# An encoder layer on one core: where w_out's operands, the second norm's vectors and the second gate's row are formed, and two operands kept as halves

## The chip, the cores and the metric

The kernel runs on one core of one Trainium2 chip. The metric is the device time of one execution in microseconds, median of several runs.

## The reference

One layer of a bidirectional encoder, in float32, over 2048 tokens of width 1024, and a final norm. Cut to what matters here:

```python
mod = silu(c) @ w_mod + b_mod                      # c: (1, 1024); w_mod: 1024 x 6144
shift1, scale1, gate1, shift2, scale2, gate2 = split(mod, 6)

h = rms_norm(x, g_norm1) * (1 + scale1) + shift1
q_a, k_a, v_a, q_m, k_m, v_m, o_m, gates = split(h @ w_in, ...)
att = rms_norm(banded_attention(q_a, k_a, v_a, sink), g_attn_out)      # 8 heads, window 128
q_m, k_m = split(silu(conv3(concat([q_m, k_m]))))
h_m = mlstm forward + mlstm backward               # 4 heads of 128, chunks of 128
h_m = sigmoid(o_m) * rms_norm(h_m, g_mlstm_out)
x = x + gate1 * (concat([att, h_m]) @ w_out)       # w_out: 1024 x 1024

hff = rms_norm(x, g_norm2) * (1 + scale2) + shift2
a, b = split(hff @ w_ffn_in, 2)                    # 1024 x 5632
x = x + gate2 * ((silu(a) * b) @ w_ffn_out)        # 2816 x 1024
return rms_norm(x, g_final)
```

## The kernel before

**Numbers as halves.** Every large product is made of three matmuls: each operand is split into a high half (rounded by ACT) and a low half (the difference, by DVE), and hi x hi, hi x lo and lo x hi are summed (`mm3`, L54 to L58). Splitting an operand of 128x1024 is one ACT and one DVE instruction. The projections through w_out and the two products of the feed-forward are written as 2 x 2 blocks with seven products instead of eight, so their operands are sums and differences of blocks, numbered 0 to 6.

**The stages, in order of time** (us of the profiled execution):
- 0 to 182, first stage: the first norm of x, 128 tokens at a time (`tt` 0 to 15), turned into `hT`; `nat_mm` computes the values and gate columns (`pa`, `pv`) of one tile in 48 matmuls. Beside this the modulation vectors are made. `mod_row(m)` sums the 1024 rows of a block of w_mod on DVE (`macc`, L373 and L375, from `wmod` tiles), splits the sum (L141, L142), adds over the partitions with two matmuls by ones (`modrow`, L381, L382), and either writes a row to memory (m = 2 and 5, the gates, into `gate_d`) or picks the columns out with DVE (m = 3 and 4, for the second norm). Row 2 is made beside tiles 4 to 7, rows 3 to 5 beside tiles 8 to 15 and behind them.
- 182 to 245, conv stage: columns of w_in (`w_first`, `w_second`, then `next_cols`) are loaded to `wraw`, split into `w0h`/`w0l` or `w1h`/`w1l` (ACT L251, POOL L254) and multiplied with hT (`gps`, L498). Two generators run beside it: `gates` (the mLSTM's gates, whose small matmuls are put at the 36th, 66th and 90th `gps` matmul by its `yield`s) and `w_out_ops`: for 8 pieces of w_out it loads two tiles, multiplies them with gate1 (POOL L944, L946), forms four differences (POOL L957) and stores the seven operands to `wo_d`.
- 245 to 570, mLSTM: for each of 4 heads a backward pass over 15 chunks and a forward pass over 16. Each chunk calls `tick()`, which runs what was put into `later` when its count is down. `prep(cc)` adds a mask on POOL (L629), `decays` takes exponentials on ACT, `k_chunk` makes `kn` and `vw`, and `kv_mm` is the product `kvp` (L622). The rest of PE's time goes to projection matmuls from the queue `fill` (`pull`).
- 570 to 815, attention, with the last projections between.
- 815 to 1004, output projection: 8 pairs of 128 tokens, each seven products of 4 steps of three matmuls (`out_proj`, `ops`). For the pair two ahead, `square` forms sums of squares (ACT L1075, POOL L1076, L1077), `columns` sums them over the partitions on PE (`aps`, L1125), `diagonal` and `scale` (PE L1088, DVE L1092) normalise the attention half, `gate` and `sums` form the operands, and `hi` and `lo` split them (L1114, L1118). w_out's operands are fetched with `start_wo(u)` (L1042) and split with `finish_wo(u)` (L1046, L1047), those of products 5 and 6 during the first pair (L1516, L1519). Behind a product DVE adds its bank to the residual (L1224).
- 1004 to 2267, feed-forward and final norm: 44 units of 84 matmuls, then the product with w_ffn_out.

**What sets the order.** PE's order is the program's from the start. In the first stage the other engines' order is made by the framework's planner from its own costs; from the conv stage to the end of the first phase of w_ffn_out it is the program's on all of them (`manual_schedule`), except in the attention. All large transfers go through SP's queue, in order, and an issue that must wait holds those behind it. A tile with one buffer under a tag is reused when its readers and its stores are done.

Of the kernel before, what the change touches and what calls it, by code (L numbers as in the profile page):

```python
# [11 lines left out]
F32 = mybir.dt.float32  # L12
# [24 lines left out]
def hybrid_layer_kernel(  # L37
# [35 lines left out]
    wo_d = dp.tile([7, 4, P, 512], F32, name="wo_d")  # L73
    a_d = dp.tile([7, DFF // P // 2, P, 2, 512], F32, name="a_d")
# [70 lines left out]
    xs, s2s = ExitStack(), ExitStack()  # L145
# [132 lines left out]
    with tc.tile_pool(name="sw", bufs=2, side="right", reuse_waits="tile") as sw:  # L278
# [80 lines left out]
        def mod_row(m):  # L359

            for z in range(2):
                acc = sw.tile([P, 512], F32, tag="macc", name="macc", bufs=1)
                if m in (2, 5):
                    br = (s1 if m == 2 else wp).tile([1, 512], F32, tag="mrow" if m == 2 else "oth", name="brow", bufs=1)
                    sp.dma_start(br, b_mod[:, m * D + z * 512:m * D + (z + 1) * 512])
                for k in range(0, KT, 2):
                    w = (hp if "b" in wrow[0] else sw if "m" in wrow[0] else wp).tile([P, 2, 512], F32, tag=wrow[0], name="wmod", bufs=1)
# [15 lines left out]
                if m in (2, 5):  # L383
                    dve.tensor_tensor(br, ps[:1, :], br, ADD)
                    sp.dma_start(gate_d[m // 5:m // 5 + 1, z * 512:(z + 1) * 512], br)
                    continue
                row = sw.tile([P, 512], F32, tag="macch", name="mrow", bufs=1)
                act.activation(row, ps, AF.Copy)
                for k in range(4):
                    rk = row[:, k * P:(k + 1) * P]  # L390
                    dve.tensor_tensor_reduce(out=rk, in0=rk, in1=ident, op0=MUL, op1=ADD, scale=1.0, scalar=0.0,
                                             accum_out=mod[:, m, 4 * z + k:4 * z + k + 1])
            if m not in (2, 5):
                o = O_BM + m * KT
                dve.tensor_tensor(mod[:, m, :], mod[:, m, :], cols[:, o:o + KT], ADD)
# [48 lines left out]
        for n in range(NB):  # L444
# [11 lines left out]
            if n + 1 == NB:  # L456
                w_first = proj_cols(C_KM)
            for i in range(4):
                tt = 4 * n + i
                if tt < 3:  # L460
# [7 lines left out]
                if tt == 8:  # L468
                    deque(nrm, 0)
                    wrow = deque(["w1h", "w1l", "wm0", "wm1"])  # L470
# [3 lines left out]
                    vecs = chain.from_iterable(mod_row(m) for m in range(3, 6))  # L474
# [9 lines left out]
                if tt != 9:  # L484
                    next(vecs, None)
# [1478 lines left out]
```

## Time and profile before

| | |
|---|---|
| median of 3 runs | 2265.35 us (2265.24 to 2266.26) |
| profiled execution | 2268.64 us |
| its span | 2266.8 us |
| PE busy | 2223.8 us, 98% |
| DVE, ACT, POOL busy | 71%, 47%, 46% |
| moved by DMA | 391 MB, 173 GB/s |

One execution is profiled; times count from the start of its span. A line of the list of waits reads: engine, tile and line that waited, `<-` what ended the wait, then the total in us, how often, and the longest. A line of the timeline reads: start, length, engine, line, operation, output `<-` inputs, shape, and in brackets how long the engine had been idle and what released it. A released-by is inferred from the latest of the events that an instruction waited for.

### The profile page before, as it was taken

What the parts mean: (1) busy time and instruction counts of PE and PEld (TensorE: products, weight loads), DVE (VectorE), ACT (ScalarE), POOL (GpSimd) and SP (SyncE); (2) the same over time, 40 slices, a digit from 0 to 9 for tenths busy, and PEclk for the clock granted to TensorE, in tenths of its full rate; (3) what the DMA queues carried; (4) which work ended last, traced back from release to release, by engine and by line L of the source; (5) the groups of instructions that cost most, each with busy time, mean ns of one, the idle gap of its engine ahead of it and who ended that gap; (6) DMA issues with size and microseconds to landing.
All of it is one profiled execution on the core that took longest, in us unless ns stands there. A gap on an engine that the chain in (4) does not pass through costs nothing.

```text
span 2266.8 us, 32424 instructions
## 1 busy us (share of the span) xinstructions
PE 2223.8 (98%) x10822; PEld 1858.7 (82%) x10822; DVE 1611.1 (71%) x2944; ACT 1060.3 (47%) x2206; POOL 1040.6 (46%) x914
## 2 busy tenths in 40 slices
PE   6999999999999999999999999999999999999998
PEld 4997888888888878888888888888888888878887
DVE  6787577656688877886767786766666665785694
ACT  5433565654677746354444444433333333233452
POOL 1006635334344333436666674457566654692020
PEclk9999999999999999999999999999999999999999
DMA  8476755586666576764343454433333374542462
GB/s 329 161 244 209 246 166 168 182 240 180 205 186 183 174 243 207 268 235 150 108 149 112 158 181 164 157 98 111 98 112 98 112 260 142 176 142 94 144 217 93
DMA packets 352811, 391.28 MB, mean 173 GB/s; under 512 B 21260, under 2 KB 251004, under 8 KB 352644
## 3 DMA queue, kind: packets, MB, share of 16 engines
q1 hardware_dynamic: 352420, 389.18, 52.6%
q8 instruction: 85, 1.39, 0.2%
q14 instruction: 82, 0.67, 0.1%
q10 hardware_dynamic: 224, 0.04, 0.0%
HBM read 269.95 MB, written 119.19 MB: 172 GB/s over the span
## 4 chain that ended last, share of the span: by engine, by line
PE 88%; DVE 4%; ACT 3%; DMA 2%; issue 1%; POOL 1%; SPq 0%; ACTq 0%; POOLq 0%; DVEq 0%
PE gps L498 14%; PE fp L56 12%; PE fp L57 12%; PE fp L58 12%; PE fo L56 6%; PE fo L58 6%; PE fo L57 6%; PE ops L56 2%; PE ops L58 2%; PE ops L57 2%; PE kvp L622 1%; PE num L709 1%; PE num L711 1%; PE atp L805 1%; ACT ap L788 1%
## 5 line engine op out<-in xcount | busy, mean ns | idle before, releaser
L498 PE MATMUL gps<-hT,whi 128*128 128x512 f32 x1088 | 396.5, 419 | 0.3 <-DVE cacc L513 0.3
L56 PE MATMUL fo<-w,ah 128*128 128x512 f32 x616 | 239.9, 389 | 1.0 <-DVE rb L1876 1.0
L58 PE MATMUL fo<-w,al 128*128 128x512 f32 x616 | 239.9, 389 | 0.1
L57 PE MATMUL fo<-w,ah 128*128 128x512 f32 x616 | 239.7, 389 | 0.0
L498 PE MATMUL gps<-hT,wlo 128*128 128x512 f32 x544 | 226.7, 417 | 0.0
L498 PEld LDWEIGHTS gps<-hT,whi 128*128 128x128 f32 x1088 | 200.2, 190 | 24.7 <-DVE cacc L513 0.7
L56 PE MATMUL fp<-T,S 128*128 128x512 f32 x528 | 206.7, 391 | 0.3 <-ACT s L1610 0.3
L57 PE MATMUL fp<-T,S 128*128 128x512 f32 x528 | 205.6, 389 | 0.0
L58 PE MATMUL fp<-T,S 128*128 128x512 f32 x528 | 205.4, 389 | 0.0
L1718 DVE TENSOR_TENSOR al<-al,ah 128x1024 fp32r<-128x1024 f32 x77 | 117.4, 1530 | 108.0 <-ACT ah L1717 108.0
L1717 ACT ACTIVATE ah<-al 128x1024 fp32r<-128x1024 f32 x77 | 81.6, 1060 | 182.8 <-DMA al<-a_d 180.3
L1453 DVE TENSOR_TENSOR S<-sf,S 128x512 fp32r<-128x512 f32 x86 | 129.8, 1547 | 34.4 <-ACT S L1452 34.2
L1453 DVE TENSOR_TENSOR A<-graw,A 128x512 fp32r<-128x512 f32 x86 | 130.8, 1541 | 13.2 <-ACT A L1452 12.8
L58 PE MATMUL fp<-B,A 128*128 128x512 f32 x352 | 136.9, 389 | 0.0
L56 PE MATMUL fp<-B,A 128*128 128x512 f32 x352 | 136.9, 389 | 0.0
L57 PE MATMUL fp<-B,A 128*128 128x512 f32 x352 | 136.9, 389 | 0.0
L56 PEld LDWEIGHTS fo<-w,ah 128*128 128x128 f32 x616 | 115.6, 188 | 25.4 <-DVE rb L1876 1.8
L58 PEld LDWEIGHTS fo<-w,al 128*128 128x128 f32 x616 | 115.6, 188 | 24.7 <-DVE al L1718 0.5
L57 PEld LDWEIGHTS fo<-w,ah 128*128 128x128 f32 x616 | 115.6, 188 | 24.2
L1620 DVE SCALAR_TENSOR_TENSOR g<-t,g 128x512 f32<-128x512 f32 x44 | 41.8, 950 | 131.3 <-ACT t L1619 131.3
L798 POOL TENSOR_SCALAR ap<-ap,adn 128x384 f32<-128x384 f32 (+1 forms) x128 | 73.5, 594 | 125.7 <-PE atp L805 58.6
L1457 POOL TENSOR_TENSOR sf<-A,A22r 128x512 f32<-128x512 f32 x42 | 58.1, 1383 | 145.5 <-DMA A22r<-in_w_ffn_in_dram 118.5
(427 smaller groups left out, 6142.2 us busy)
## 6 DMA issues: line engine op xcount, KB each, us to landing
al<-a_d SPq DMA_DIRECT2D x77, 512.0 KB, 3.8
wmod<-in_w_mod_dram SPq DMA_DIRECT2D x48, 512.0 KB, 7.6
graw<-in_w_ffn_in_dram SPq DMA_DIRECT2D x43, 512.0 KB, 3.9
a_d<-ka SPq DMA_DIRECT2D x66, 256.0 KB, 4.7
bc<-bc_d SPq DMA_DIRECT2D x64, 256.0 KB, 3.7
hop_d<-n SPq DMA_DIRECT2D x56, 256.0 KB, 4.0
a_d<-u SPq DMA_DIRECT2D x55, 256.0 KB, 4.6
mqk<-qk_d SPq DMA_DIRECT2D x44, 256.0 KB, 3.8
```

The costliest lines, as they stand in the source:

```text
L56: pe.matmul(o, lh, rh, start=first, stop=False, skip_group_check=skip)
L57: pe.matmul(o, lh, rl, start=False, stop=False, skip_group_check=skip)
L58: pe.matmul(o, ll, rh, start=False, stop=last, skip_group_check=skip)
L498: pe.matmul(ps, w[i == 2][:, k, :], hT[n](i == 1, k), start=(k == 0 and i == 0), stop=(k == KT - 1 and i == 2))
L622: pe.matmul(kvp[:, :129], kn, vw, start=True, stop=True)
L709: pe.matmul(num[:, d, :129], sc[:, d, :], va_c, start=True, stop=st is None)
L798: pool.tensor_scalar(self.p[g][:, :self.NK], self.p[g][:, :self.NK], dn[:, g:g + 1], 0.0, MUL, ADD)
L1453: dve.tensor_tensor(t[:, 1, :], f, t[:, 0, :].bitcast(F32), SUB)
L1457: add.tensor_tensor(f1, a21, a22, ADD)
L1620: dve.scalar_tensor_tensor(g0, t0, 1.0, g0, ADD, MUL)
L1717: act.activation(ah, al.bitcast(F32), AF.Copy)
L1718: dve.tensor_tensor(al, al.bitcast(F32), ah.bitcast(F32), SUB)
```

## The change

It moves three pieces of work and rearranges what they touch.

- **w_out.** `w_out_ops` moves from the conv stage into the first stage, beside tiles 9 to 12, in four rounds over full rows instead of eight over half rows. It uses the tags of the projection weights: w_out rows in `wm0`/`wm1` (even rounds) and `w0h`/`w0l` (odd rounds), the differences in `w1h` (`ta`) and `w1l` (`tb`). The gain `g_attn_out` is multiplied into w_out's rows here (ACT), so `scale` in the output projection no longer has it. `w_first` is emitted at tile 14 instead of 12.
- **Halves.** The operands of products 4 and 6 are split before they are stored (a high half in `wo_d`, a low half in the new `wol_d`), and are loaded as two halves. The order of loads and splits before and in the first pair of the output projection changes with it, the squares are taken at step 9 instead of 15, and the pool `xd` opens at step 22 instead of 14.
- **The second norm's vectors** (rows 3 and 4) are formed in the mLSTM, a quarter row at a time: `late_vecs` loads 128x2x256 pieces into the tag `oth`, sums on DVE four ticks later, and `vec_columns` does the two matmuls, of 256 columns. `prep(0)` and `prep(1)` move from the end of the backward pass into its chunks 3 and 1.
- **The second gate's row** (row 5) is formed by `gate2` in the feed-forward's second half, one step in each unit.
- The steps of `gates` are put at matmul 46, 80 and 104 instead of 36, 66 and 90.

```diff
-            vecs = chain.from_iterable(mod_row(m) for m in range(3, 6))
+            wx = wxs.enter_context(tc.tile_pool(name="wx", bufs=1, side="left", reuse_waits="tile"))
+            gb = wx.tile([P, 2, 512], F32, name="gb")
+            sp.dma_start(gb.rearrange("p m c -> p (m c)"), gate_d[0, :].partition_broadcast(P))
+            vecs = w_out_all()
...
+        def w_out_ops(k, b):
+            bx, by = b
+            act.activation(bx, bx, AF.Copy, scale=cols[:, O_GA + k:O_GA + k + 1])
+            for t in (bx, by):
+                pool.tensor_tensor(t, t, gb, MUL)
+            ta = wp.tile([P, 2, 512], F32, tag="w1h", name="ta", bufs=1)
+            tb = wp.tile([P, 2, 512], F32R, tag="w1l", name="tb", bufs=1)
+            hi = wx.tile([P, 2, 512], F32R, name="tbh")
+            tf = tb.bitcast(F32)
+            sp.dma_start(wo_d[0, k], bx[:, 0])
+            sp.dma_start(wo_d[1:6:4, k].rearrange("u p c -> p u c"), by)
+            for t, f, g in ((ta[:, 1], bx[:, 1], bx[:, 0]), (tf[:, 0], by[:, 1], bx[:, 1]),
+                            (ta[:, 0], by[:, 1], ta[:, 1]), (tf[:, 1], by[:, 0], ta[:, 0])):
+                pool.tensor_tensor(t, f, g, SUB)
+            sp.dma_start(wo_d[2:4, k].rearrange("u p c -> p u c"), ta)
+            act.activation(hi, tf, AF.Copy)
+            dve.tensor_tensor(tb, tf, hi.bitcast(F32), SUB)
+            sp.dma_start(wo_d[4:7:2, k].rearrange("u p c -> p u c"), hi.bitcast(F32))
+            sp.dma_start(wol_d[:, k].rearrange("u p c -> p u c"), tf)
+
+        def w_out_load(k):
+            r = [pl.tile([P, 2, 512], F32, tag=tag, name="wox", bufs=1)
+                 for pl, tag in (((sw, "wm0"), (sw, "wm1")), ((wp, "w0h"), (wp, "w0l")))[k % 2]]
+            for t, k_ in zip(r, (k, k + 4)):
+                sp.dma_start(t, w_out[k_ * P:(k_ + 1) * P].rearrange("p (m c) -> p m c", m=2))
+            return r
+
+        def w_out_all():
+            b = [w_out_load(0), w_out_load(1)]
+            for k in range(4):
+                yield True
+                w_out_ops(k, b[k])
+                if k < 2:
+                    b.append(w_out_load(k + 2))
...
+    def late_vecs():
+        for m in (3, 4):
+            for q in range(4):
+                acc = s2.tile([P, 256], F32, tag="lacc", name="lacc", bufs=1)
...
+                for k in range(0, KT, 2):
+                    w = wp.tile([P, 2, 256], F32, tag="oth", name="wmod", bufs=1)
+                    sp.dma_start(w, w_mod[k * P:(k + 2) * P, m * D + q * 256:m * D + (q + 1) * 256]
+                                 .rearrange("(k p) c -> p k c", p=P))
+                    yield 3
+                    for i in range(2):
+                        if k + i == 0:
+                            dve.tensor_scalar(acc, w[:, 0, :], sc_col[:, 0:1], None, MUL)
+                        else:
+                            dve.scalar_tensor_tensor(acc, w[:, i, :], sc_col[:, k + i:k + i + 1], acc, MUL, ADD)
+                split(acc, hi, lo)
+                later.append([1, lambda m=m, q=q, hi=hi, lo=lo: vec_columns(m, q, hi, lo)])
...
+            if cc in (3, 1):
+                prep(1 - cc // 2)
...
-        prep(0)
-        prep(1)
         decays(0)
...
-            for k in range(4):
-                dve.scalar_tensor_tensor(self.a[:, :, k], self.a[:, :, k], cols[:, O_GA + k:O_GA + k + 1], rb, MUL, MUL)
+            dve.tensor_tensor(self.a, self.a, rb.unsqueeze(2).to_broadcast([P, 2, 4, P]), MUL)
...
-    finish_wo(2)
     finish_fill(lasts[2])
-    for u in (4, 5):
-        start_wo(u)
-    xr.append(load_xr(nxt.tt + 1))
+    start_wo(5)
+    nx2.load_gate()
     nx3.load_a()
-    finish_wo(3)
+    xr.append(load_xr(nxt.tt + 1))
+    start_wo(4)
+    finish_wo(2)
     pull(26)
     for _ in range(2):
         nxt.both()
-    finish_wo(4)
+    finish_wo(3)
...
+    HI0, LO0 = (5, 13, 18, 20, 22, 24, 26), (5, 15, 18, 20, 22, 24, 26)
...
-                if i in (6, 14):
-                    for hi, lo in zip(*wo[5 + i // 14]):
+                if i == 6:
+                    for hi, lo in zip(*wo[5]):
                         act.activation(hi, lo.bitcast(F32), AF.Copy)
-                if i in (8, 16):
-                    for hi, lo in zip(*wo[4 + i // 8]):
-                        dve.tensor_tensor(lo, lo.bitcast(F32), hi.bitcast(F32), SUB)
-                if i in (3, 12, 13):
+                if i in (8, 11):
+                    hi, lo = (t[i // 11] for t in wo[5])
+                    dve.tensor_tensor(lo, lo.bitcast(F32), hi.bitcast(F32), SUB)
+                if i in (0, 2, 13):
                     cur.both()
-                if i == 14:
+                if i == 22:
...
-                if i == (1 if p else 15):
+                if i == (1 if p else 9):
...
+        def gate2():
+            row = lambda n, dt=F32: ff.tile([P, D], dt, tag="xt", name=n, bufs=4)
...
+            for k in range(KT):
+                if k + 1 < KT:
+                    fetch(k + 1)
+                if k == 0:
+                    dve.tensor_scalar(acc, wr[0], sc_col[:, 0:1], None, MUL)
+                else:
+                    dve.scalar_tensor_tensor(acc, wr[k % 2], sc_col[:, k:k + 1], acc, MUL, ADD)
+                yield True
```

More of the change, by code (lines that the diff above doesn't have):

```diff
@@ L967, in hybrid_layer_kernel @@
     w_second = proj_cols(C_QM)
     win = ExitStack()
-    steps = [gates(), w_out_ops()]
-    due = [0, next(steps[1])]
+    steps = [gates()]
+    due = [0]
     win.enter_context(tc.manual_schedule(engines={getattr(mybir.EngineType, e) for e in ("DVE", "Activation", "Pool", "SP")}))
@@ L1248, in hybrid_layer_kernel @@
         start_wo(u)
+    xr = [load_xr(nxt.tt)]
+    nx2.load_m()
     pull(10)
@@ L1525, in hybrid_layer_kernel @@
             if nx2:
-                if i == (1 if p else 15):
-                    sq = [xd.tile([P, 512], F32, tag="n2", name="msq", bufs=9).rearrange("p (k t) -> p k t", k=4) for _ in range(2)]
+                if i == (1 if p else 9):
+                    sq = [(xd.tile([P, 512], F32, tag="n2", name="msq", bufs=9) if p else
+                           w1.tile([P, 512], F32, tag="sq", name="msq")).rearrange("p (k t) -> p k t", k=4) for _ in range(2)]
                     for j in range(2):
@@ L1696, in beside @@
                     norms.popleft()
+                if n > NJ and u == 1:
+                    next(gate, None)
             pair(hh, j, ws_, hop, start, beside, turn)
```

165 lines of the change are left out of this document (73 added, 92 removed).

## The prediction

> **What bounds the kernel now.** I read the page first, then PE's busy time and granted clock by stretch, then the list of waits of PE, then the instructions around each place where PE stands.
>
> ```profile
> span 2266.8 us, 32424 instructions
> PE 2223.8 (98%) x10822; PEld 1858.7 (82%) x10822; DVE 1611.1 (71%) x2944; ACT 1060.3 (47%) x2206; POOL 1040.6 (46%) x914
> ```
>
> PE is busy for 2223.8 of 2266.8 us, so 43 us are all that can be won without taking matmuls away, and the change takes few away. The profiled execution took 2268.64 us, of which 2266.8 are span; the median of the runs shown is 2265.35, 3.3 us less. I make the sum as a difference and put it on the median.
>
> ```profile
> 123.00:175.00 52.00, 50.63 (x328) 48.60 (x327) 43.44 (x102) 13.54 (x30) 4.34 (x10) 1.00 0.89 284
> 175.00:182.00 7.00, 5.02 (x27) 4.32 (x26) 3.81 (x8) 2.51 (x5) 2.08 (x3) 1.00 0.39 113
> 182.00:186.00 4.00, 4.00 (x12) 3.11 (x11) 2.56 (x7) 2.35 (x5) 1.26 (x2) 0.57 0.46 148
> 245.00:570.00 325.00, 322.88 (x1892) 276.79 (x1891) 219.26 (x769) 182.45 (x580) 139.12 (x186) 1.00 0.63 189
> 815.00:828.00 13.00, 13.00 (x60) 10.61 (x59) 11.71 (x16) 5.00 (x8) 1.60 (x2) 1.00 0.92 311
> 828.00:841.00 13.00, 8.22 (x26) 6.08 (x25) 9.59 (x22) 6.44 (x11) 8.16 (x7) 0.74 0.17 50
> 1000.00:2000.00 1000.00, 999.61 (x4437) 826.47 (x4436) 695.35 (x667) 402.63 (x675) 611.96 (x385) 1.00 0.42 140
> ```
>
> The columns after the length are busy time and count of PE, PEld, DVE, ACT and POOL, then the granted clock, the DMA share and GB/s. Two places that the change touches are poor: the end of the first stage (175 to 186, with a clock of 0.57 behind the stand) and the first pair of the output projection (828 to 841: 26 matmuls in 13 us at 0.74, where 815 to 828 has 60). The feed-forward, 1000 to 2000, has PE idle for 0.4 us in 1000.
>
> ```profile
> PE aps L1125 <- POOL msq L1077: 3.2, 2, 2.1
> PE modrow L381 <- ACT macch L141: 2.2, 2, 1.6
> PE ops L56 <- ACT msq L1075: 1.6, 1, 1.6
> PE kvp L622 <- ACT vw L617: 1.2, 1, 1.2
> ```
>
> The largest of these waits behind the start-up are those of `modrow` in the first stage, one of `kvp` in the mLSTM, and `aps` and `ops` in the projection. The change edits the cause of each.
>
> **A: the first stage.** The sums for modulation rows 3 to 5 leave tiles 9 to 15, six pairs of `modrow` matmuls and their waits with them.
>
> ```profile
> 137.45 0.40 PE L381 MATMUL modrow<-macch,ones_r 128*128 128x512 f32 x1
> 137.91 0.29 PE L56 MATMUL pa<-wnh,hT 128*128 128x272 f32 x1
> 138.04 0.28 PE L57 MATMUL pa<-wnl,hT 128*128 128x272 f32 x1
> 145.12 0.39 PE L381 MATMUL modrow<-macch,ones_r 128*128 128x512 f32 x1
> 181.72 0.93 PE L498 MATMUL gps<-hT,whi 128*128 128x512 f32 x2
> ```
>
> A pair in a full stream costs 137.91 - 137.45 = 0.46 us. A tile without one takes 145.12 - 137.91 = 7.21 us, and five tiles follow 137.45, so PE could be done with the stage at 137.45 + 5 x 7.21 = 173.5, and begin `gps` there: 8.1 us before 181.6 (181.72 less the two gate transposes). Without a stand the clock would be kept too: the 12 matmuls of 182 to 186 took 4.0 us at 0.57 and take 12 x 0.225 = 2.7 at the spacing of 1000 to 2000 (4437 in 1000 us), 1.3 less.
>
> What decides is when `gps` gets its first weights. They use the tags `w0h` and `w0l`, in which the change now holds the w_out rows of k = 3, so w_first waits for the last round of `w_out_ops`. It was free of that before.
>
> ```profile
> L944 POOL TENSOR_TENSOR bx<-bx,gb 128x512 f32<-128x512 f32 x8 | 11.3, 1407 | 12.2 <-DMA bx<-in_w_out_dram 6.4 <-PE gps L498 5.8
> 189.07 1.30 POOL L944 TENSOR_TENSOR bx<-bx,gb 128x512 f32<-128x512 f32 x1 [5.80 <-PE gps L498]
> L254 POOL TENSOR_TENSOR wlo<-wraw,whi 128x256 fp32r<-128x256 f32 x68 | 51.0, 772 | 45.9 <-ACT whi L251 35.6 <-PE kvp L622 9.7 <-DMA qst_d<-qhi 0.3
> 178.79 1.06 ACT L251 ACTIVATE whi<-wraw 128x1024 fp32r<-128x1024 f32 x1 [0.32 <-DMA wraw<-in_w_in_dram]
> 830.92 1.21 DVE L1519 TENSOR_TENSOR wo<-wo 128x1024 fp32r<-128x1024 f32 x1
> wmod<-in_w_mod_dram SPq DMA_DIRECT2D x48, 512.0 KB, 7.6
> wo_d<-ts SPq DMA_DIRECT2D x8, 256.0 KB, 4.4
> 123.75 0.94 SPq L369 DMA_DIRECT2D wmod<-in_w_mod_dram  x2
> ```
>
> A round on POOL is two products of 128x1024 (2 x 1.30 less a little, 2.55 each) and four differences of 128x512 (1.30 each): 10.3 us. Single buffers link the rounds: the second difference writes `tb`, which is free when the round before has split it (ACT 1.06, DVE 1.21) and its store has landed (L). So a round takes the larger of 10.3 and 3 x 1.30 + 1.06 + 1.21 + L = 6.2 + L. With L = 4.4 that is 10.6, with 7.6 it is 13.8. I take L = 6.0, between, because the stage now moves some 17 MB (4.2 of w_out, 0.5 of the gate, 9.4 of stores, about 3 of the rest) where 123 to 175 moved 14.8 at a share of 0.89. Rounds are 12.2 us.
>
> The rows and the gate (1.57 MB, 5.5 us at 284 GB/s) are issued where the first `wmod` of this part was, at 123.75, and are there at 129.3; with ACT's scaling (1.06) POOL begins at 130.4 and ends round 0 at 140.7, round 3 at 140.7 + 3 x 12.2 = 177.3. `whi` can be made a little before that, the first quarter of `wlo` takes 0.77 more: `gps` at 178.1, 4.6 us behind PE's end of the stage. So **A = 178.1 - 181.6 = -3.5 us**, with the lower clock behind the stand as before. Its ends: -9.4 (no stand, clock kept) and, for rounds bound by slow stores, the rival below. Behind w_first stands w_second, whose slots `w1h` and `w1l` are the last round's `ta` and `tb`; it has 96 matmuls, 22 us, of cover. The gate chain's steps are put 10 to 14 matmuls later, 3 us, and the mLSTM, which reads its result, begins at about 245; that costs nothing.
>
> The row for 182 to 186 shows the clock low behind a stand in which the longest listed wait is 1.6 us. The Trainium skill (TensorE: Matmul & The Clock Gate, Part 1) has the clock halved after an idle window of about 3.4 us; by it a stand short of that would keep the clock, and A would gain up to 1.3 us more, an estimate. The trace has it halved behind less, so the sum does not use it.
>
> What leaves the conv stage with `w_out_ops` (POOL, SP) was beside PE; no gain is booked.
>
> **B: the first pair of the projection.**
>
> ```profile
> 815.16 2.35 DVE L1047 TENSOR_TENSOR wo<-wo 128x1024 fp32r<-128x1024 f32 x2
> 819.31 1.65 DVE L1092 SCALAR_TENSOR_TENSOR ma<-ma,cols,arb 128x256 f32<-128x256 f32 x4
> 829.14 0.39 PE L58 MATMUL ops<-wo,mS 128*128 128x512 f32 x1
> 828.71 1.69 DVE L1118 TENSOR_TENSOR mA<-mm,mA 128x512 fp32r<-128x512 f32 x2 [0.62 <-ACT mA L1114]
> 830.32 0.67 DVE L1224 TENSOR_TENSOR xr<-xr,ops 128x512 f32<-128x512 f32 x1
> 831.14 0.47 PE L56 MATMUL ops<-wo,mS 128*128 128x512 f32 x1 [1.61 <-ACT msq L1075]
> 832.79 1.32 POOL L1077 TENSOR_TENSOR msq<-msq 128x128 f32<-128x128 f32 x1
> 834.16 0.58 PE L1125 MATMUL aps<-ones_r,msq 128*128 128x1 f32 x2 [2.09 <-POOL msq L1077]
> 816.42 2.58 SPq L1042 DMA_DIRECT2D wo<-wo_d  x2
> ```
>
> PE stops at step 20 (product 5 into the bank of product 3). The wait is put down to ACT's `msq`, but what it needs is DVE's addition of product 3, which reads that bank: it begins at 830.32, ends at 830.99, and PE goes on at 831.14. DVE was late because it splits wo[4] (2.35 us, from 815.16) in the same queue. Then PE stops twice for POOL's `msq`, made from squares put at step 15. After the change wo[4] and wo[6] come from memory as halves, so 2.35 us go from ahead of that addition and another pair of splits from behind it; `scale` is one instruction of 1024 columns (about 1.21 for 1.65); the second operand's low half (about 0.85 of 1.69) stands behind the addition. 2.35 + 0.4 + 0.85 = 3.6 us earlier: it ends near 827.4, before PE is ready for it (829.14 + 0.23). The squares are at step 9 and out of `xd`'s way, six steps of 0.69, 4 us, earlier, and POOL has little else there (1.60 us busy in 815 to 828). So both waits go, and the lower clock with them. 828 to 841 holds 22 matmuls of 0.23 and 4 short ones of 0.15, 5.7 us of work in 13: **B = -7.3 us**.
>
> What could be late next is data: two operands' loads are doubled, 2.1 MB more, 6.7 us at the 311 GB/s of 815 to 828. wo[6] is issued at 816.4; with a landing of 7.6 and those 6.7 it is there by 830.7; PE, on time, needs it at step 24, 829.37 + 4 x 0.69 + 0.6 = 832.7. Two us are left.
>
> **C and D: the mLSTM and the feed-forward.**
>
> ```profile
> 340.47 0.73 POOL L254 TENSOR_TENSOR wlo<-wraw,whi 128x256 fp32r<-128x256 f32 x1 [9.71 <-PE kvp L622]
> 341.16 1.42 POOL L629 TENSOR_TENSOR ng<-bc,maskb 128x256 f32<-128x256 f32 x2
> 343.14 0.49 PE L622 MATMUL kvp<-vw,kn 128*128 128x129 f32 x2 [1.22 <-ACT vw L617]
> 342.73 0.42 DVE L681 SCALAR_TENSOR_TENSOR sc<-sps,ng 128x256 f32<-128x256 f32 x1 [1.91 <-ACT ng L635]
> ```
>
> The wait of 1.22 us at a head's turn is a chain: `ng` on POOL stands behind a `wlo`, ACT's exponentials behind `ng`, `vw` behind those, PE behind `vw`. `prep` is now made several chunks earlier: **C = -1.2 us**.
>
> Rows 3 and 4 now run in quarters: 8 pairs of matmuls over 256 columns in a stage where PE is 99% busy. A pair costs between 0.26 (two matmuls of 272 columns, 138.04 - 137.91 = 0.13 apart) and the 0.46 of a 512-column pair; nearest is between, 0.33: +2.6. Row 5 is two pairs of 512 columns in the feed-forward, +0.9. **D = +3.5 us** (2.9 to 4.6).
>
> DVE gets 64 products of 128x256 (0.42 each, 27 us) and some 10 us of splits and reductions in 325 us: from 219 to 256 us busy, 79%. Each product waits for a transfer of 256 KB issued four ticks earlier, and behind it on DVE stand the state updates on which PE waits two chunks later; SP has 32 more issues among the mLSTM's own. I book **+0.5 us**, ends 0 and 8. The eight products of 128x1024 in the feed-forward, 1.21 each, one in each block of 84 matmuls (19.4 us), fall where DVE has 30% free and PE waits for nothing: 0.
>
> **The sum.** -3.5 - 7.3 - 1.2 + 3.5 + 0.5 = -8.0 us: 2260.6 for the profiled execution, 2257.4 on the median.
>
> **The rivals.** No stand in the first stage: rounds at 10.6 us, as with L = 4.4, end at 172.5, the weights are there at 173.3, A is -9.4 and the time 2251.5. For it: the 4.4 row. Against: the stage's DMA share of 0.89.
>
> Slower: the rounds are bound by their stores. The sum is zero where `gps` starts 4.5 us later than before, at 186.1, which is rounds of 14.9 us, L = 8.7. At L = 11 rounds are 17.2, round 3 ends at 192.3 and `gps` starts at 193.1, 11.5 late: -7.3 - 1.2 + 4.0 + 11.5 = +7.0, 2272.4. For it: 7.6 us of landing for `wmod`, and more bytes now. Against: the bytes needed by then, 15.5 MB without the last round's stores, at the 319 GB/s that a full share makes of 284, have gone by 172. Two engines also get in each other's way: L944 has a mean of 1.41 us where one undisturbed takes 1.30. The Trainium skill (SBUF — State Buffer, Who interferes with whom) says that a VectorE instruction with two SBUF inputs and a GpSimd one that reads SBUF exclude each other for a whole instruction; were each of a round's six operations held up by one of 0.67 us, rounds would be 14.3, `gps` would start at 188.4, and the sum would be +2.3, an estimate. The trace bears out a tenth of that, and VectorE's sums leave the stage.
>
> The wait in the projection only moves: wo[6] lands 3 to 4 us late or DVE's queue is still behind at step 20, so that B is -3.5 and the time 2261.2. For it: DVE is busy for 11.71 of 13 us there.
>
> That the mLSTM's late products hold DVE for their transfers: 32 waits, half of them with 0.5 us on PE, +8, time 2264.9.
>
> **How the numbers follow.** Forecast 0.50; no stand 0.16; slow stores 0.15; moved wait 0.12; mLSTM waits 0.07. A difference of 0.2% is 4.5 us, so faster means below 2260.8 and slower above 2269.9; that is about what a measurement here can tell. Faster: 0.46 of the forecast's 0.50 (the rest has larger rounds), 0.16, and 0.05 of the moved wait: 0.67. Slower: 0.13 of the slow stores and 0.03 of combinations: 0.16. Same: 0.17. The range is from the first rival's time, less 1, to 2267, which leaves out the slow stores beyond L = 9.
>
> **What would show it.** Right: `gps` L498 starts between 173.5 and 180; no PE wait for `ops` or `aps` in the first pair and a clock of 1.00 there; no 1.2 us wait of `kvp`; the busy time of PE in the mLSTM up by some 3 us. Wrong: `gps` standing behind `whi` or `wlo` beyond 186, DVE's addition of product 3 still ending after PE's step 19, or DVE waiting for `wmod` in the mLSTM with PE behind it.

## The result and the profile after

The changed kernel takes 2306.39 us (median of 5 runs, 2301.69 to 2308.62), the kernel before, beside it, 2266.26 us: a ratio of 1.0174, 95% interval 1.0163 to 1.0186. It is 40 us slower where 8 us faster was forecast. The profiled execution took 2303.5 us.

The first two lines of its page, then busy time and granted clock by stretch, with the columns of the prediction's table:

```profile
span 2301.7 us, 32337 instructions
PE 2230.5 (97%) x10830; PEld 1864.5 (81%) x10830; DVE 1612.6 (70%) x2953; ACT 1062.3 (46%) x2217; POOL 1042.0 (45%) x890
```
```profile
123.00:175.00 52.00, 39.70 (x247) 39.07 (x246) 9.92 (x15) 12.37 (x22) 40.97 (x28) 0.87 0.74 262
190.00:245.00 55.00, 55.00 (x247) 44.80 (x246) 27.96 (x64) 24.08 (x53) 8.55 (x12) 1.00 0.28 89
250.00:610.00 360.00, 334.70 (x1896) 282.79 (x1895) 261.52 (x874) 184.32 (x589) 137.87 (x179) 0.98 0.62 190
856.00:869.00 13.00, 13.00 (x60) 10.69 (x59) 9.46 (x11) 5.73 (x9) 3.70 (x4) 1.00 1.02 356
869.00:882.00 13.00, 12.59 (x59) 9.89 (x59) 10.05 (x25) 4.80 (x9) 6.70 (x5) 1.00 0.73 242
1040.00:2040.00 1000.00, 999.52 (x4437) 826.68 (x4436) 701.60 (x676) 401.68 (x674) 618.81 (x388) 1.00 0.43 144
```

PE's busy time is 6.7 us more and the span 34.9. The first pair of the output projection, 13 us with 26 matmuls before, now has 59. The mLSTM, which had PE idle for 2.1 of 325 us, has it idle for 25.3 of 360, with a clock of 0.98, which is some 7 more, an estimate (2% of 360). In the first stage PE stands for 12.3 us.

Three rows of PE by tile mark the stages: the first `gps`, the first `kvp` and the last `num` (behind the counts: least, median and greatest duration in ns, first and last start).

```profile
L525 PE MATMUL gps<-hT,whi x1088: 387/395/778, 188.8 to 856.2; 128*128 128x512 f32 x182
L691 PE MATMUL kvp<-vw,kn x240: 271/274/581, 250.0 to 601.6; 128*128 128x129 f32 x120
L778 PE MATMUL num<-mv,sc x256: 271/273/422, 274.1 to 609.8; 128*128 128x129 f32 x128
```

Cut at these marks, and at the first `fp` of the feed-forward, every kernel of this study splits into five stretches (us, from the profiled execution of each):

| kernel | first gps | conv | mLSTM | num to fp | from fp | span |
|---|---|---|---|---|---|---|
| before | 181.7 | 63.6 | 322.4 | 422.9 | 1276.2 | 2266.8 |
| changed | 188.8 | 61.2 | **359.8** | 416.6 | 1275.3 | 2301.7 |
| difference | +7.1 | -2.4 | **+37.4** | -6.3 | -0.9 | +34.9 |

Each figure is of one execution. Ten kernels of this study share the changed kernel's first stage: nine have `gps` at 188.7 to 189.7 and one at 192.3. The stretch from `fp`, the same in all the changed kernels, varies by 3.5 us. So a few us in one stretch can be chance; the conv stage, 61.2 us in all nine kernels that have it as changed, is steadier.

Who waits for whom in the changed kernel: PE's own waits, and between 250 and 610 us those of ACT, DVE and SP's queue behind them (in total, times, longest).

```profile
PE kvp L691 <- ACT vw L686: 14.4, 8, 4.8
PE pa L56 <- ACT va L509: 12.3, 2, 10.9
PE ktp L681 <- DMA mqk<-qk_d: 5.0, 3, 2.4
PE ops L56 <- ACT mA L1137: 1.4, 1, 1.4
```
```profile
ACT lhi L142 <- DVE lacc L638: 22.8, 8, 4.5
DVE lacc L638 <- DMA wmod<-in_w_mod_dram: 6.8, 5, 2.9
```
```profile
SPq L631 <- DVE sc L750: 42.2, 11, 7.1
SPq L631 <- DVE lacc L638: 28.4, 11, 7.0
SPq L631 <- DVE cb L731: 20.6, 8, 4.1
SPq L631 <- DMA wmod<-in_w_mod_dram: 15.8, 10, 2.9
```

`aps` is gone from PE's list and `ops` has 1.4 us left, in another pair. Two new things stand out in the mLSTM. ACT waits 8 times, once for each quarter row, to split a sum that DVE has not finished. PE stands right behind every one of these: four times at `kvp` (11.6 of the 14.4 us), once for 1.9 us at `ktp` and three times for under 1 us. The other four waits of `kvp`, 2.8 us, are not behind a split. And SP's queue stands 107 us at the load of `wmod` (L631). Such a sum is no price: in the kernel before, SP stands 100.6 us at the loads of `bc` (L603), and PE is idle for 2.1 us in that whole stage. This is the largest of ACT's eight stands, engine by engine:

```profile
398.04 0.69 ACT L806 ACTIVATE og<-htp,gml 128x512 f32<-128x512 f32 x1 [1.24 <-PE htp L804]
401.23 0.35 DVE L789 TENSOR_SCALAR hst<-num,rd 128x128 f32<-128x128 f32 x1
401.88 1.28 DVE L638 SCALAR_TENSOR_TENSOR lacc<-wmod,sc_col,lacc 128x256 f32<-128x256 f32 x2
403.20 0.42 ACT L142 ACTIVATE lhi<-lacc 128x256 fp32r<-128x256 f32 x1 [4.48 <-DVE lacc L638]
403.52 0.39 ACT L686 ACTIVATE vw<-mv,wT 128x129 f32<-128x129 f32 x1
403.20 0.38 SPq L631 DMA_DIRECT2D wmod<-in_w_mod_dram  x1
403.97 0.80 PE L691 MATMUL kvp<-vw,kn 128*128 128x129 f32 x2 [4.82 <-ACT vw L686]
```

A tick (the head of a chunk, where `later` is run) puts the quarter's last two products on DVE and at once, behind them in program order, the split on ACT and the next load on SP. DVE is still at work on what was put there earlier: without a pause since 395.1 it does the small steps of a norm, two steps of the convolution and, for the chunk before, `hst`. So it comes to the products at 401.88. ACT has been at the split since 398.7, with nothing else allowed past it; the new chunk's `vw` runs 0.3 us after the split, and PE, which needs `vw` early in the chunk, has stood 4.8 us. The Trainium skill (Perfetto Trace Analysis, Tensor Engine Instruction) calls ACT, DVE and GpSimd strictly first in, first out; these rows agree.

The first stage has the same picture. ACT there:

```profile
131.06 0.47 ACT L510 ACTIVATE va<-pv 128x384 f32<-128x384 f32 x1
140.84 1.06 ACT L402 ACTIVATE tbh<-tb 128x1024 fp32r<-128x1024 f32 x1 [9.32 <-POOL tb L400]
143.00 0.47 ACT L510 ACTIVATE va<-pv 128x384 f32<-128x384 f32 x1
151.50 1.06 ACT L402 ACTIVATE tbh<-tb 128x1024 fp32r<-128x1024 f32 x1 [8.03 <-POOL tb L400]
155.18 0.28 ACT L509 ACTIVATE va<-pa 128x128 f32<-128x128 f32 x1 [2.46 <-DVE gn L508]
155.50 0.59 PE L56 MATMUL pa<-wnh,hT 128*128 128x272 f32 x1 [10.93 <-ACT va L509]
```

The planner put the split of a round's differences (L402) ahead of the evacuation of PE's finished banks, ACT waited 9.3 and 8.0 us for POOL, and PE had no free bank. The clock is low behind PE's stand:

```profile
155.00:160.00 5.00, 4.50 (x20) 4.50 (x21) 0.14 (x2) 0.77 (x2) 4.10 (x4) 0.50 0.86 237
```

From 175 on PE has no stand in this stage, and `gps` follows tile 15 at once.

### The profile page after: what moved, and what is told of

It is laid out like the page before. It is cut to its first block, busy times and chain, and to the rows that moved or that the text cites. A ratio compares the mean times of both kernels' runs of the same rounds, so it can differ in the third digit from the quotient of the medians.

```text
span 2301.7 us, 32337 instructions
## 1 busy us (share of the span) xinstructions
PE 2230.5 (97%) x10830; PEld 1864.5 (81%) x10830; DVE 1612.6 (70%) x2953; ACT 1062.3 (46%) x2217; POOL 1042.0 (45%) x890
## 4 chain that ended last, share of the span: by engine, by line
PE 58%; DVE 2%; issue 0%; DMA 0%; ACT 0%; SPq 0%; ACTq 0%
PE fp L56 12%; PE fp L57 12%; PE fp L58 12%; PE fo L58 5%; PE fo L56 5%; PE fo L57 5%; PE ops L56 2%; PE ops L58 2%; PE ops L57 2%; DVE al L1775 1%; DVE ra L1918 1%; DVE w L1784 0%; DMA al<-a_d 0%; PE trn L184 0%; PE trn L1333 0%
## 5 line engine op out<-in xcount | busy, mean ns | idle before, releaser
L1475 DVE TENSOR_TENSOR S<-sf,S 128x512 fp32r<-128x512 f32 x86 | 124.5, 1485 | 36.9 <-ACT S L1474 36.8
L1475 DVE TENSOR_TENSOR A<-graw,A 128x512 fp32r<-128x512 f32 x86 | 126.3, 1488 | 15.8 <-ACT A L1474 15.5
```

The costliest lines, as they stand in the source:

```text
L1475: dve.tensor_tensor(t[:, 1, :], f, t[:, 0, :].bitcast(F32), SUB)
```

## The experiments

The theories. In the mLSTM: **S**, ACT stands at the split and `vw` behind it; **Q**, SP stands at the load, and `mqk`, `mv` and `bc` behind it come late; **V**, the added products themselves hold DVE; **P**, the mask additions put earlier hold POOL. In the first stage: **E**, the planner's order holds PE's banks; **R**, the rounds on POOL set the time. Ratios are to the kernel before, beside each run.

**Which edit it is.** Setting rows 3 and 4 to zero, putting `prep` back, and issuing the load a tick later:

```diff
-    go_late()
+    dve.memset(mod[:, 3:5, :], 0.0)
+    dve.scalar_tensor_tensor(gs2, mod[:, 4, :], 1.0, cols[:, O_G2:O_G2 + KT], ADD, MUL)
```


> Leaves out the vectors of rows 3 and 4 (they are set to zero): no wmod loads, no products, no modrow matmuls in the mLSTM. All that is left of the change there is the earlier prep. Theory Q and theory V: mLSTM at 318-324 us, as before the change or shorter, whole about 2262-2268, which is +7 for the first stage, -2.4 conv stage, -6.6 projection and 0 for the mLSTM against before. Theory P: mLSTM stays above 340 us, whole above 2285.

2269.27 us, 1.0007 [0.9997, 1.0016], 1.3 us above the expected range; mLSTM 322.6. The vectors are the whole of the 37 us, and the earlier `prep` gains nothing (322.4 before).

```diff
-            if cc in (3, 1):
-                prep(1 - cc // 2)
...
+        prep(0)
+        prep(1)
         decays(0)
```


> Puts prep(0) and prep(1) back to the end of the backward pass; all else as changed. Theory P: mLSTM falls by 20 us or more, whole below 2285. Theories Q and V: within 5 us of the changed kernel, 2301-2311.

2306.2 us, 1.0173 [1.0158, 1.0188]; mLSTM 360.2. P is out.

```diff
                 for k in range(0, KT, 2):
+                    if m + q + k > 3:
+                        yield 0
                     w = wp.tile([P, 2, 256], F32, tag="oth", name="wmod", bufs=1)
...
-                    yield 3
+                    yield 2 if m + q + k > 3 else 3
```


> Same work and same transfers as the changed kernel; only the next load of wmod is issued one tick after the two products that free its slot, instead of directly behind them, and the pace of four ticks a step stays. Theory Q (SP's queue stands at the wmod load until DVE has got through its products, and the loads of bc, mqk and mv behind it come late): the mLSTM, from the first kvp to the last num, falls from 359.8 us to 325-335, the whole to 2267-2280, and the 108 us that the changed kernel's SP waits at L631 fall under 25. Theory V (DVE is held by the added products themselves): mLSTM stays above 350, whole above 2295. Theory P (the mask additions put earlier block POOL): mLSTM stays above 350 as well.

2307.31 us, 1.0174 [1.0153, 1.0195]; mLSTM 365.2: as a test of Q a miss. SP's wait at that line only fell from 107 to 59 us, where under 25 was expected, so the edit did not take away what it was to take away. The stands at the split were still there (26.9 us in all).

**Split and transfers apart.**

```diff
+                yield 0
                 split(acc, hi, lo)
```


> One line more in the changed kernel: the split of a quarter's sum is issued one tick after the quarter's last two products, not directly behind them. Theory S (ACT reaches the split, stands until DVE has got to those two products, and vw and with it kvp stand behind it): the waits of ACT lhi for DVE lacc, 22.8 us in 8 times, fall under 5, PE's 14.4 us of kvp for ACT's vw fall under 6, the mLSTM falls from 359.8 us to 335-348 and the whole to 2281-2295. Theory V (DVE held by the added products themselves): mLSTM within 5 us of 359.8, whole above 2300.

2286.9 us, 1.0085 [1.007, 1.01]; mLSTM 342.7, 17.1 less by one line, as S said. (The line also puts the next quarter's first load a tick later; the run above did that with the other 31 loads and gained nothing.) In the lists of waits:

```profile
ACT lhi L142 <- DVE lacc L638: 4.5, 3, 2.1
PE kvp L692 <- ACT vw L687: 1.4, 4, 0.8
```

The 22.8 and 14.4 us of the changed kernel are down to 4.5 and 1.4.

```diff
-                    w = wp.tile([P, 2, 256], F32, tag="oth", name="wmod", bufs=1)
-                    sp.dma_start(w, ...)
+                    if m + q + k == 3:
+                        w = wp.tile([P, 2, 256], F32, tag="oth", name="wmod", bufs=1)
+                        sp.dma_start(w, ...)
```


> Leaves out 31 of the 32 loads of wmod in the mLSTM: all 64 products read the first tile, at their old places (the sums are not those of the reference). No transfer, no issue and no wait of SP at that line is left. Theory Q (SP's queue and the transfers): mLSTM at 325-335 us, whole 2270-2282. Theories S and V (ACT's split, or DVE's products): mLSTM above 345, whole above 2292.

2294.46 us, 1.0125 [1.0109, 1.014]; mLSTM 351.4, 8.4 less. Transfers and SP's queue are a second, smaller cause; ACT's eight stands stay:

```profile
ACT lhi L142 <- DVE lacc L639: 27.2, 8, 4.5
```

The profiled execution was the longest of this kernel's four, 5.9 us above their median, so 8.4 may be too little. Both edits together (`yield 0` and the one load):

> The changed kernel with both single edits: the split one tick later, and 31 of 32 loads of wmod left out (sums not those of the reference); products at their places at the head of a chunk, in all passes. Each edit alone took 17.1 and 8.4 us off the mLSTM's 359.8. If the two causes are separate, the mLSTM comes to 332-337 us and the whole to 2277-2284; if one of them only uncovers the other, to 340-343 (2286-2290); if together they are all of it, to 325-328 (2270-2275).

2276.97 us, 1.0045 [1.003, 1.006]; mLSTM 332.4, which is 27.4 less, where the two alone add to 25.5. By the medians, each less the kernel before beside it, the two edits alone are worth 20.5 and 13.0 us and both together 30.1. Either way they about add up: the causes are separate. What is left over the kernel without vectors is 9.8 us: PE's matmuls, 3.3 us in which PE stands at `modrow` for the later split, and products at the head of a chunk.

**The same work at other places.** All 32 steps in the forward passes, behind `sc` and the state update; products one chunk behind their load, split and `modrow` later still:

```diff
                 if kv:
                     state(cc, kv)
+            next(late, None)
             pull(nf - 6)
```


> All 32 steps moved into the forward passes and to the middle of a chunk, behind sc and the state update: load in one chunk, the two products in the next, the split with the next quarter's first load, modrow one chunk behind it. The same work. Nothing stands then at the head of a chunk, so by theory S and by theory Q the mLSTM is at 322-332 us (322.4 before the change and 3 for PE's matmuls), whole 2266-2280. By theory V, the same 27 us of products now in 250 us instead of 325, it stays above 345, whole above 2292.

2284.11 us, 1.0072 [1.0057, 1.0087]; mLSTM 336.0, between the two expectations. DVE's list shows what was left:

```profile
DVE lacc L643 <- DMA wmod<-in_w_mod_dram: 17.1, 12, 3.7
```

One chunk, some 4 us, is too short a lead for the load, and DVE, in order, holds all behind it (PE waits 6.4 us for `vw` here). With the one load of above:

> The forward-only order once more, with 31 of the 32 loads of wmod left out (all products read the first tile, so the sums are not those of the reference). In the forward-only kernel the mLSTM still took 336.0 us, 13.4 more than without the vectors, and DVE stood 17.1 us for wmod. If the transfers (one chunk of lead) are what is left, the mLSTM comes to 325-329 us and the whole to 2271-2277. If DVE's products are, it stays at 333-337 and the whole at 2280-2286.

2274.2 us, 1.0028 [1.0018, 1.0038]; mLSTM 327.8: 8.2 of the 13.4 us were the short lead, and the products cost little once they are not at the head of a chunk. V falls as the main cause. Then row 3 in the conv stage and row 4 in the forward passes, each load two steps or two chunks ahead:

```diff
+    early = early_vecs()
     for i in range(2 * 96 + 60):
+        if i > 6 and i % 6 == 0:
+            next(early, None)
```


> Row 3 is formed in the conv stage, where DVE was busy for 28 of 55 us and the DMA share was 0.28, with two steps of lead for each load; row 4 in the forward passes, a load four chunks apart, its products two chunks behind it, in the middle of a chunk, the split one chunk behind those. All else as changed. Expected: conv stage 61.2 + 1.3 us, mLSTM 323-328, whole 2269-2276. If added products cost whatever their order, the mLSTM stays above 331.

2270.67 us, 1.0015 [1.0006, 1.0024]; conv stage 62.6, mLSTM 324.1. That is 1.4 and 1.5 us more than without the vectors (61.2 and 322.6), for four pairs of `modrow` each: 0.36 us a pair, inside the 0.26 to 0.46 of the prediction. The same 64 products and 32 transfers cost 3 us instead of 37, no more than their matmuls. PE is idle in its mLSTM for 1.5 of 324 us:

```profile
251.00:575.00 324.00, 322.53 (x1887) 275.37 (x1885) 239.19 (x818) 182.48 (x581) 136.28 (x179) 1.00 0.67 199
```

**The first stage.** The split left out:

```diff
-            act.activation(hi, tf, AF.Copy)
-            dve.tensor_tensor(tb, tf, hi.bitcast(F32), SUB)
-            sp.dma_start(wo_d[4:7:2, k]..., hi.bitcast(F32))
+            sp.dma_start(wo_d[4:7:2, k]..., tf)
```


> Leaves out the split of the operands of products 4 and 6 (the whole values are stored in place of both halves): ACT and DVE have no instruction left in the first stage that waits for a difference of POOL. All stores stay. Theory E (the splits, put ahead of PSUM evacuations in ACT's and DVE's order, hold PE's banks): PE's wait of 12.3 us for pa goes, PE busy in 123 to 175 is above 50 us, the last product of tile 15 ends at 174-177 us, and gps starts at 178-182 instead of 188.8, held by w_first alone; whole 7-10 us less than the changed kernel, about 2297. Theory R (the rounds on POOL set the time, whoever splits): gps stays above 186 and the whole within 3 us of the changed kernel.

2302.62 us, 1.0151 [1.0135, 1.0168]; `gps` at 180.8, 8.0 earlier, as E said, but the mLSTM took 366.3 and gave most of it back. Why the mLSTM was longer is not traced. PE's wait in the first stage did not go, it halved (6.9 us), now behind another of ACT's instructions for the rounds, the scaling of rows not yet loaded:

```profile
146.20 1.15 ACT L389 ACTIVATE wox<-wox,cols 128x1024 f32<-128x1024 f32 x1 [9.50 <-DMA wox<-in_w_out_dram]
149.96 0.59 PE L56 MATMUL pa<-wnh,hT 128*128 128x272 f32 x1 [6.72 <-ACT va L506]
```

Then nothing left out, but the order of ACT, DVE, POOL and SP from tile 8 on written by hand (in short: which steps follow which tile's evacuation; the small `memset` of `va` also goes from POOL to DVE):

```diff
+                    by_hand.enter_context(tc.manual_schedule(engines=others))
...
+            0: scale 0, ops 0; 1: scale 1, put 0; 2: split 0, ops 1; 3: put 1, load 3, scale 2;
+            4: split 1, ops 2, put 2; 5: scale 3, split 2, ops 3; 6: put 3; 7: split 3
```


> The same work as the changed kernel; from tile 8 on the order of ACT, DVE, POOL and SP is written out by hand: tile evacuations first, a round's split put behind the evacuation of a later tile, w_first's raw load behind tile 12. POOL's rounds are the same four. Theory E (the planner's order is what holds PE): no wait for pa, PE ends tile 15 at 174-176 us, POOL's last round ends at 172-175, gps starts at 174-178, 11 to 15 us earlier than in the changed kernel, and with the mLSTM as it is the whole is 2290-2297. Theory R (rounds bound by POOL and stores): gps stays above 183.

2298.47 us, 1.0136 [1.0119, 1.0153]; `gps` at 177.6, 11.2 earlier: E explains the loss, not R. The whole is a little above its range, as the conv stage took 64.6. The wait for `pa` is gone. One of 4.4 us for the last tile's `gn` took its place, since `whi` of w_first stood on ACT ahead of tile 15's evacuation. And there the rounds come in: `whi` takes the slot of the last round's rows and waited for POOL:

```profile
175.53 1.06 ACT L252 ACTIVATE whi<-wraw 128x1024 fp32r<-128x1024 f32 x1 [5.23 <-POOL tb L401]
177.22 0.69 PE L928 MATMUL gps<-ident,gn 128*128 128x128 f32 x2 [4.41 <-DVE va L526]
```

A second order, with one product of a round on DVE and stores and splits earlier:

```diff
-            for t in (by, bx):
-                pool.tensor_tensor(t, t, gb, MUL)
+            pool.tensor_tensor(bx, bx, gb, MUL)
...
+            dve.tensor_tensor(rows_[k][1], rows_[k][1], gb, MUL)
```


> The first stage by hand, second version: one of the two products of a round on DVE, a round's difference and half stores issued as soon as they are ready, the split one or two tiles behind its round, w_first's weights behind the last of them and ahead of tile 15's evacuation no longer waiting for the rows. By theory E gps starts at 173-176 us (177.6 in the first version), the conv stage takes 61-63, and with the mLSTM as changed the whole is 2290-2296.

2298.3 us, 1.0132 [1.0117, 1.0147]; `gps` at 180.4, later than the first order, a miss: ACT's `vs` has one buffer and now stood for its store.

**Both together.** The second hand-written order with rows 3 and 4 as above:

> Both together: the first stage by hand, row 3 in the conv stage, row 4 in the forward passes; w_out's operands, the halves and the second gate as changed. Sum from the stages of the runs so far against the kernel before: gps at 174.5 instead of 181.7 (-7), conv stage 62.5 for 63.6 (-1), mLSTM 326 for 322.4 (+4), projection -6, feed-forward -1: 2267 - 11 = 2256. If the two orders disturb each other or the mLSTM keeps 13 us, 2262 to 2268.

2261.82 us, 0.9973 [0.9962, 0.9984], 5.9 us under the kernel before beside it (2267.69). Its stretches are 178.6, 63.9, 324.5, 416.8 and 1274.9. It beats both kernels, by less than the sum of 2256 said, as `gps` came at 178.6 and not 174.5.

Then a tile's stores on ACT's queue instead of SP's, and DVE's `gn` taken from the bank ahead of ACT's `vs` (two edits in one run):

```diff
+                dve.tensor_tensor(gn[..., tt], pa[:, 128:144]..., bgv, ADD)
                 act.activation(vs[:, :, 0, :], pav, AF.Copy)
...
-                dve.tensor_tensor(gn[..., tt], pa[:, 128:144]..., bgv, ADD)
...
-                sp.dma_start(vst_d[...], vs.bitcast(F32))
-                sp.dma_start(vaug_d[...], va)
+                q_ = sp if tt < 8 else act
+                q_.dma_start(vst_d[...], vs.bitcast(F32))
+                q_.dma_start(vaug_d[...], va)
```


> The combined kernel; from tile 8 on the two stores of a tile's values are issued on ACT's queue instead of SP's, and gn is taken from PSUM ahead of vs. In the combined kernel ACT's vs waited for the store of the tile before, which stood in SP's queue behind w_out's stores, and PE waited 3.2 us for gn at the end of the stage. If that queue is what is left of the first stage's stand, gps starts at 173.5-176 instead of 178.6, as early as PE ends tile 15, and the whole is 2256-2260, 2 to 5 us less than the combined kernel. If POOL's rounds are (the last difference at 173.2), gps stays at 177.5-179 and the whole at 2260-2263.

2268.56 us, 1.0005 [0.9995, 1.0014], worse than the combined kernel. `gps` came only 1.0 earlier, and the conv stage took 70.1:

```profile
185.85 1.06 ACT L252 ACTIVATE whi<-wraw 128x1024 fp32r<-128x1024 f32 x1 [6.37 <-DMA wmod<-in_w_mod_dram]
186.81 0.26 ACT L970 ACTIVATE gates<-gps 128x128 f32<-128x128 f32 x1
194.38 0.77 PE L1001 MATMUL rps<-ident,gates 128*1 128x128 f32 x4 [4.43 <-DVE gates L996]
```

The same fault a third time: ACT at a transfer, the gates' chain behind it, PE behind that. With the second weight columns loaded at their turn in the conv stage:

```diff
-    w_second = proj_cols(C_QM)
...
-    ready.extend((w_first, w_second))
-    coming.extend(c0 + h * P for h in range(1, HM) for c0 in (C_KM, C_QM))
+    ready.append(w_first)
+    coming.extend([C_QM] + [c0 + h * P for h in range(1, HM) for c0 in (C_KM, C_QM)])
```


> The kernel with the values' stores on ACT's queue; the second weight columns are loaded and split like all later ones, at their turn in the conv stage, and no longer right behind the first stage. There, ACT stood 6.4 us for those columns ahead of the gates' copies, and PE 4.4 us for the gates. If that was all of its loss, the conv stage falls from 70.1 us to 61-63.5, and the whole to 2258-2262. If the queue itself costs, the conv stage stays above 66 and the whole above 2264.

2259.79 us (2259.07 to 2261.41), 0.9971 [0.996, 0.9982], the lowest here, though not told apart from the combined kernel's 0.9973; `gps` at 175.9, conv stage 62.4. The stand was all of the loss. And with the stores back on SP's queue and `gn` back behind `vs`:

> The same edit in the combined kernel, where the gates' copies came ahead of that wait: conv stage 62.5-64 us instead of 63.9, gps at 178-179, whole 2259-2262, the same as the combined kernel within 2 us.

2262.77 us, 0.9985 [0.9974, 0.9996]; conv stage 64.4, `gps` at 179.7. All three are a little above what was expected. So with that stand away the stores on ACT's queue and the earlier `gn` are together worth 3.8 us of `gps`, and 3.0 by the medians; no run has one without the other. Its feed-forward was longer (1278.4 from the first `fp`, against 1275.0; not traced further).

## Why the prediction was wrong, point by point

- **The term for the mLSTM's DVE and SP load is the step that failed.** It was booked at +0.5 with ends 0 and 8, and measured some +35: 37.4 less the 2.6 that D counts for matmuls. Busy time was added up (79% of DVE forecast; 261.5 of 360 us is 73%; a product took 0.49 us for 0.42), and transfers were counted as issues. Which engine reaches a waiting instruction first, and what stands behind it there, was not asked. The prediction named what stands behind DVE and counted SP's issues; ACT's half of `split` was nowhere in it: 17.1 us. The load, whose slot is free only when DVE has read it and which lands only some time after, was the other 8.4; how much of this is SP's stands and how much DVE's waits for the transfer, no run tells apart. Last, a chunk whose critical `vw`, `sc` and state update come early in each engine's order has little room at its head. With both causes removed 9.8 us were left, matmuls among them; with the products in the middle of a forward chunk, and the loads left out there too, 5.2.
- **The rival for that term** (mLSTM waits, +8, chance 0.07) had the place and the smaller part of the mechanism. It put DVE at the transfer; DVE's waits for `wmod` are 6.8 us in the changed kernel, ACT's for DVE 22.8. That its 8 is near the 8.4 of the loads is partly luck, as those hold SP's stands too.
- **A: the model of the rounds was right, its condition wrong.** `gps` was forecast at 178.1 and came at 188.8. The rounds were not late:

```profile
128.69 4.76 POOL L391 TENSOR_TENSOR wox<-wox,gb 128x1024 f32<-128x1024 f32 x2 [2.26 <-DMA gb<-gate_d]
171.51 1.29 POOL L400 TENSOR_TENSOR tb<-wox,ta 128x512 f32<-128x512 f32 x1
```

  Four rounds from 128.7 to 172.8 are 11.0 us each, and the last ended 4.5 us before its forecast, 1.7 of them by an earlier start. Late was PE's own end of the stage, taken at 173.5 with nothing in its way: 12.3 us of stands, and some 3 for the clock behind them (0.50 from 155 to 160, 0.88 from 160 to 165; an estimate), make 188.8. That the estimate for two engines in each other's way (188.4) and the slow-store rival (186.1 to 193.1) lie round this time is luck, as the rounds were short. What was missing is that ACT's split and scaling stand in the same queue as the evacuation of PE's banks, in an order that a planner chose. With that order written by hand the condition was met, and the model held: rounds of 12.2 us from 127.8 to 176.7, a stand of 4.4 us where 4.6 was taken, and `gps` at 177.6, 0.5 us from the forecast. (One figure against the slow stores does not add up: 17 MB without the last round's stores, a quarter of 9.4, are 14.7 and not 15.5; the conclusion drawn from it stands.)
- **B held.** With the second gate, -7.3 + 0.9 = -6.4 was forecast for all behind the attention; the stretch from the last `num` to the first `fp` is 6.3 shorter and the feed-forward 0.9. Neither `ops` nor `aps` waits in the first pair, and its clock is 1.00. The rival that the wait only moves (-3.5) is out. B was not run alone; it is read from the stages: in 14 of the 16 experiments, all of which keep it, that stretch is 5.1 to 6.4 us shorter than before, in the two that left the vectors or the split out 3.7 and 3.5.
- **C gained nothing** where 1.2 was booked: without the vectors the mLSTM takes 322.6 with the earlier `prep`, against 322.4 before, and 360.2 against 359.8 with the vectors when it is put back. Without the vectors the `kvp` wait of 1.2 us became 0.64 us, and one of 0.5 us for `mqk` is new.
- **D's pair of 256 columns** was taken at 0.33 us and comes out at 0.36, if all that rows 3 and 4 add in the order with early and late rows is matmuls. The second gate's cost in the feed-forward (0.9) is not seen: 1276.2 before, 1275.3 after, which is inside what that stretch varies.
- **The conv stage**, booked at nothing, gained 2.4. The low clock behind the stand ahead of it, which A took as kept, went; that is 1.3 by A's own working. The rest is not traced.

## What to carry to other kernels

When work is slipped beside a stage whose engines look 20 to 50% idle, follow each added instruction on its own queue: if it can be reached before what it needs is done, everything behind it on that engine waits, and PE with it. Put the producer and the consumer at least a step apart on different engines, give a load time to land before its reader, and put both behind the instructions that the next matmul needs. A busy share says whether the work fits; only the place and the order say what it costs: here 37 us or 3 for the same work.

## What the runs showed of the hardware

DVE and POOL held each other up more than the prediction allowed. DVE's low half of a split (two inputs of 128x1024 from SBUF) took 1.22 us while POOL was idle and 2.3 beside POOL. A difference of POOL's took 1.29 us alone and 2.26 beside that split. These are rows of the changed kernel's first stage:

```profile
140.77 2.41 POOL L391 TENSOR_TENSOR wox<-wox,gb 128x1024 f32<-128x1024 f32 x1
141.94 2.32 DVE L403 TENSOR_TENSOR tb<-tb,tbh 128x1024 fp32r<-128x1024 f32 x1 [15.26 <-ACT tbh L402]
143.12 2.26 POOL L400 TENSOR_TENSOR ta<-wox 128x512 f32<-128x512 f32 x1
161.79 1.22 DVE L403 TENSOR_TENSOR tb<-tb,tbh 128x1024 fp32r<-128x1024 f32 x1 [6.65 <-ACT tbh L402]
```

DVE ends 1.1 us after POOL's product has ended, and POOL's difference ends 1.1 us after DVE has: not far from the 1.22 and 1.29 that each takes alone, as if each had waited for the other's instruction to end. The Trainium skill (SBUF — State Buffer, Who interferes with whom) has the two hold each other up for a whole instruction, and these rows agree; the prediction had seen a tenth of it in the kernel before and set the rule aside. In the first stage it cost two of the four rounds about 1 us each and decided nothing. In the mLSTM it has a part in the backlog behind which ACT's largest stand lies: there three small steps of the norm take 0.59 to 0.66 us beside POOL, where the same steps just before took 0.16:

```profile
397.17 0.59 DVE L105 TENSOR_TENSOR mra<-mry 128x4 f32<-128x4 f32 x1
397.79 0.65 DVE L106 TENSOR_TENSOR mra<-mra,mrh 128x4 f32<-128x4 f32 x1
398.48 0.66 DVE L107 SCALAR_TENSOR_TENSOR mry<-mra,mry 128x4 f32<-128x4 f32 x1
396.99 0.75 POOL L698 TENSOR_TENSOR ng<-bc,maskb 128x256 f32<-128x256 f32 x1 [1.26 <-DVE mra L106]
397.70 1.42 POOL L255 TENSOR_TENSOR wlo<-wraw,whi 128x256 fp32r<-128x256 f32 x2
```

That is 1.4 us of the 4.5, an estimate; no run takes it away.
